# Softmax values computed with the tokens on the partitions, at the head of each attention layer

## The chip, the cores and the metric

The kernel runs on one core of one Trainium2 chip. The metric is the device time of one execution in microseconds (us). A core has TensorE (PE in the profile, its weight loads PEld), VectorE (DVE), ScalarE (ACT), GpSimd (POOL) and SyncE (SP), which here only issues DMAs.

## The reference

A transformer trunk of two layers on 512 tokens of width 1024, in float32:

```python
for l in range(DEPTH):                              # 2
    h = rmsnorm(x, attn_norm[l])
    sb_q, sb_k, sb_v, df_q, df_k, df_v = jnp.split(h @ w_in[l], splits, axis=-1)   # six times 512 columns
    sb_out = stick_breaking_attention(sb_q, sb_k, sb_v)          # 8 heads of 64
    dq, dk = rope(df_q, pos), rope(df_k, pos)
    df_heads = differential_attention(dq, dk, dvv, lam)          # 4 heads: two softmax maps of 64, values of 128
    df_out = rmsnorm(df_heads, subln_norm[l]) * (1.0 - lambda_init)
    x = x + concat([sb_out, df_out]) @ w_o[l]
    h = rmsnorm(x, mlp_norm[l])
    x = x + square(relu(h @ w_ff1[l])) @ w_ff2[l]                # 4096 wide
return rmsnorm(x, final_norm)
```

## The kernel before, in words

**Numbers in two parts.** Every float32 operand of a matmul is split into a high part, which ACT rounds, and a low part, which DVE gets by subtraction (`split`, `W.split_part`, `make_h`). A product of two such operands is a *triple* of matmuls: high times high, high times low, low times high (`three`, lines 278 to 283). The weights' splits show in the profile as `whi` (L116) and `wlo` (L117), the activations' as `h_hi` (L228) and `h_lo` (L229).

**Layout.** x lies transposed, with the 1024 features in eight chunks on the partitions and the 512 tokens along the free axis. `h` is x times the norm's gain only; the factor per token of the RMS norm is multiplied in when a projection leaves PSUM. For that, `add_sq` squares the chunks (ACT) and sums them (DVE) into `ssq`; `rms_a` transposes `ssq` on PE (`rs_a`), reduces it to `rcol`, one factor for each token on the partitions, and `rms_b` spreads it (`rb_a`) to `rbc`, the same factors along the free axis of all partitions. Cosine and sine tables are multiplied with `rbc` once.

**Weights.** They come in units of 128x1024, through a ring of three raw buffers filled by SP's queue in the order of `_UNITS`, and are split into one of two slots (four in the MLP). A unit's split can begin when its slot's former unit has been used up.

**Projections.** `dense` walks through `ORDER`. Item `d` is one softmax head's query and key (two units), `s` two stick-breaking heads' query and key, `u` the values of two stick-breaking heads and `w` those of one softmax head. Each unit gives a *block*: eight triples, one for each chunk, with the weights stationary and 512 tokens moving, into one PSUM bank. So a value block has features on the partitions; `evict_v` multiplies it with `rbc` (DVE), transposes it on PE (L374, `vT`), and splits it (L381, L382) into `vs` or `vd_hi`, `vd_lo`, which attention reads with tokens on the partitions.

**The opening of a layer.** In layer 0, the two units of `d0` are computed chunk by chunk as x arrives, into two banks. In layer 1, x's chunks come out of layer 0's MLP, where they lie with tokens on the partitions: `back` transposes a chunk on PE (L872, `yT`), adds it to x (L873, DVE) and makes `h`; then the same two units of `d0` are computed chunk by chunk (lines 1023 to 1041), with the squares behind them.

**Order.** Instructions go to each engine's queue in an order that a scheduler derives at compile time from the order of the program, letting later ready instructions pass. Within an attention layer the program's order is made by a planner (lines 729 to 747): it keeps a clock of estimated PE time, 0.648 us a triple, and after every dense triple spends a credit on pieces of attention (`attn`): scores S, transposes T of the weights, outputs O, for 8 units of softmax heads and then 16 of stick-breaking heads. Credit is what is left of attention (`ATT`, 54 us) over what is left of the dense work (`DENSE`, 145 us), at most `CAP`. Attention may touch a head `DLY_R` + `DLY_D` (3.5 + 8 us) after a `d` block's eviction, `DLY_S` (6 us) after an `s` block's. These delays stand for the splits and for the small DMAs that copy queries and keys into stacks (`move`, L408, on SP's queue: twelve for a `d`, six for an `s`). Steps count triples: `rms_a` is issued at step `RA`, `rms_b` at `RB`; before `RB` no block is evicted, and the blocks are held in PSUM. The dense work ends with `wo(1)`, the half of the output projection that reads softmax heads; `wo(0)`, which reads the stick-breaking heads, comes when attention is done.

**MLP.** Four groups; in each, eight blocks `f` and then seven sums of matmuls ("forms", with two banks each), which are a Strassen scheme for the second matrix. PSUM has eight banks, given out under four tags: `t` 2, `mm` 2, `s` 3, `o` 1.

Of the kernel before, what the change touches and what calls it, by code (L numbers as in the profile page):

```python
# [30 lines left out]
ORDER = ("d0", "w0", "d1", "w1", "d2", "w2", "d3", "w3", "s0", "u0", "s1", "u1", "s2", "u2", "s3", "u3")  # L31
# [5 lines left out]
RA, RB, DLY_V = (21, 20), (32, 31), 3.5  # L37
# [3 lines left out]
TAIL, ATT, DENSE, CAP = 6.0, 54.0, 145.0, 0.1  # L41
# [8 lines left out]
def _unit_list():  # L50
# [5 lines left out]
    for l in range(L):  # L56
        for item in ORDER:
            b = int(item[1])
            if item[0] == "d":
                units.append(("x", l, b, 0))  # L60
                units.append(("x", l, b, 1))
            elif item[0] == "s":
                qk(l, SBQ, SBK, b)
            else:
                units.append(("p", l, (SBV if item[0] == "u" else DFV) + b * P))
# [86 lines left out]
def trunk(ctx, tc, xT, w, w2, gains, gfin, lamv, cos, sin, out):  # L152
# [39 lines left out]
    W.loaded = 2  # L192
    W.load(3)
# [103 lines left out]

    def constants(a2):
# [18 lines left out]
    for l in range(L):  # L317
        with ExitStack() as actx:
# [27 lines left out]
            if l == 0:  # L346
                for c in range(KC):
                    if c % 2 == 0:
                        for i in range(2):
                            W.split_part(i, c * P, (c + 2) * P)  # L350
                    opened = make_h(c, gcol("attn", 0, c))
                W.split = 2
                for i in range(2):
                    W.home[2 + i] = tuple(
                        m[:, 2 * i : 2 * i + 2, :].rearrange("p e t -> p (e t)") for m in (md_hi, md_lo))
                squares = [add_sq(c, c == 0, tt, nc.vector) for c in range(KC)]
# [4 lines left out]
                W.do_split(3)  # L361
                behind(squares[2][0], W.last[0])
                behind(squares[2][1], W.last[1])
                W.do_split(4)
                constants(a2)

            def evict_v(pt, kind, b, which):
# [3 lines left out]
                def rest():  # L371
                    tv = bank("s" if kind == "u" else "t", f"vT{l}{kind}{b}")
                    for tb in range(4):
                        nc.tensor.transpose(tv[:, tb * P : (tb + 1) * P], t[:, tb * P : (tb + 1) * P], ident)  # L374
                    if kind == "u":
                        hi, lo = (vs[:, :, 2 * b : 2 * b + 2, a : a + 64] for a in (0, 64))
                        src = tv.rearrange("p (t h e) -> p t h e", t=4, h=2)
                    else:
                        hi, lo = (v[:, :, b * P : (b + 1) * P] for v in (vd_hi, vd_lo))
                        src = tv.rearrange("p (t e) -> p t e", t=4)  # L380
                    nc.scalar.activation(hi, src, AF.Copy)  # L381
                    nc.vector.tensor_tensor(out=lo, in0=src, in1=hi.bitcast(F32), op=ALU.subtract)  # L382
                    ready[("vs" if kind == "u" else "vd", b)] = clock[0] + 1.5

                defer(DLY_V, rest)

# [311 lines left out]
            def dense():  # L698
                pts = opened_by.pop() if l else None
                if l == 0:  # L700
                    us = [W.next("x"), W.next("x")]
                    pts = [bank("mm", f"p{l}{i}") for i in range(2)]
                    turns = [(c, i) for c in range(5) for i in range(2)] + [(c, i) for i in range(2) for c in (5, 6, 7)]
                    for c, i in turns:
                        three(pts[i], wpair(us[i], c), hpair(c), c == 0, c == KC - 1)
                        yield 3 * 0.216
                step, b = 2 * KC, int(ORDER[0][1])
                held = [(pts[0], "d", b, "q"), (pts[1], "d", b, "k")]
                for item in ORDER[1:]:
                    kind, b = item[0], int(item[1])  # L710
                    for which in ("qk" if kind in "ds" else "v"):
                        name = f"p{l}{kind}{b}{which}"
                        for pt in block(name, "s" if step in (16, 24, 32) else "mm"):
                            step += 1
                            if step == RA[l]:
                                dgs["a"] = rms_a(ssq, 1.0 / D, rcol, f"a{l}", nc.vector, tr)
                            if step == RB[l]:
                                rms_b(rbc, f"a{l}", dgs["a"])
                                nc.vector.tensor_mul(cos_t, cos_t, rbc)
                                nc.vector.tensor_mul(sin_t, sin_t, rbc)  # L720
                            yield 3 * 0.216
                        held.append((pt, kind, b, which))
                        if step >= RB[l]:
                            for args in held:
                                {"w": evict_v, "u": evict_v, "s": evict_s, "d": evict_d}[args[1]](*args)
# [4 lines left out]
            done = 2 * KC * 3 * 0.216 if l else 0.0  # L730
# [27 lines left out]
        with ExitStack() as fctx:  # L758
# [89 lines left out]

            def turned(tb, j):
# [61 lines left out]
            for g in range(GROUPS):  # L911
# [12 lines left out]
                for k in range(2 * GP):  # L924
                    for n, pt in enumerate(block(f"f{l}_{g}_{k}", "any")):
# [12 lines left out]
                for f, form in enumerate(FORMS):  # L938
                    to = [bank((("s", "s"), ("s", "o"), ("mm", "mm"))[f % 3][r], f"{form}{l}{g}{r}") for r in range(2)]
# [5 lines left out]
                    for n, (c, i, r) in enumerate(work):  # L945
# [76 lines left out]
            else:  # L1022
                W.pools.pop()
                us = [W.next("x"), W.next("x")]
# [83 lines left out]
```

## Time and profile before

| | us |
|---|---|
| median of 3 runs | 1175.3 (1173.34 to 1177.56) |
| the profiled execution | 1172.68 |
| its span, first to last instruction | 1170.9 |
| TensorE busy in it | 1147.6 |
| VectorE busy | 813.1 |
| ScalarE busy | 651.5 |
| GpSimd busy | 212.7 |

Rows of a timeline read: start, duration (both us), engine, line, operation, what it writes and reads, shape, count, and in brackets the idle time of the engine before it with what ended it. A merged row with "x2" covers two instructions. Matmuls overlap, so that a single one lasts longer than the distance to the next. Rows of waits read: who waited, for whom, us in total, times, longest. In the chain of work, a piece is counted only for the time in which it holds up the end.

### The profile page before, as it was taken

Reading aid. Unit: us, or ns where it says so; the run is one execution under the profiler, and the core shown is the slowest. Engines: PE = TensorE matmul, PEld = TensorE weight load, DVE = VectorE, ACT = ScalarE, POOL = GpSimd, SP = SyncE. Lnnn points to the kernel's source line nnn. Section 1 sums busy time; section 2 is a strip of 40 time slices with the busy share of each in tenths; the row PEclk is TensorE's granted clock in tenths of the full one; section 3 lists DMA queues with packets and bytes.
Section 4 is the critical chain, followed back from the end, with each engine's and each line's share of the span. In section 5 each row is a group of like instructions: output and inputs, shape, how many; then the busy total and the mean of one; then the engine's idle time right before and its main releaser. Section 6 shows DMA issues by size and latency. Waiting matters only on the chain.

```text
span 1170.9 us, 15335 instructions
## 1 busy us (share of the span) xinstructions
PE 1147.6 (98%) x5454; PEld 951.2 (81%) x5454; DVE 813.1 (69%) x1302; ACT 651.5 (56%) x1153; POOL 212.7 (18%) x282
## 2 busy tenths in 40 slices
PE   9999999999999999999899999999999999999996
PEld 6787888888888888888677878888888888888885
DVE  7888788765545746647778887877664466475568
ACT  6455666556656446455445555655666564554554
POOL 1222443130100101002012215331201010010021
PEclk9999999999999999999999999999999999999999
DMA  7555333255844936727416553432548357276185
GB/s 243 158 156 172 119 116 108 72 189 153 196 149 108 229 123 125 222 96 159 106 54 190 153 161 109 125 110 72 216 120 224 128 127 228 93 148 210 36 175 132
DMA packets 56860, 170.11 MB, mean 145 GB/s; under 512 B 7120, under 2 KB 8144, under 8 KB 56784
## 3 DMA queue, kind: packets, MB, share of 16 engines
q1 hardware_dynamic: 46416, 131.88, 34.0%
q0 software_dynamic: 10224, 37.23, 18.0%
q8 instruction: 43, 0.70, 0.2%
q14 instruction: 33, 0.27, 0.1%
q10 hardware_dynamic: 144, 0.02, 0.0%
HBM read 138.17 MB, written 2.10 MB: 120 GB/s over the span
## 4 chain that ended last, share of the span: by engine, by line
PE 86%; DVE 5%; DMA 2%; issue 2%; ACT 1%; POOL 0%; SPq 0%; POOLq 0%; DVEq 0%; ACTq 0%
PE f L283 10%; PE f L281 10%; PE f L282 10%; PE x L281 4%; PE x L283 4%; PE x L282 4%; PE wo L281 3%; PE wo L283 3%; PE wo L282 3%; DMA q<-in_w 2%; DVE wlo L117 1%; PE T1s L555 1%; PE T0s L555 1%; PE O0s L584 0%; PE O1s L584 0%
## 5 line engine op out<-in xcount | busy, mean ns | idle before, releaser
L117 DVE TENSOR_TENSOR wlo<-raw,whi 128x1024 fp32r<-128x1024 f32 (+1 forms) x132 | 157.0, 1193 | 95.6 <-ACT whi L116 95.0
L117 DVE TENSOR_TENSOR wlo<-q,whi 128x512 fp32r<-128x512 f32 x224 | 145.9, 687 | 108.6 <-ACT whi L116 108.1
L281 PE MATMUL f<-h_hi,whi 128*128 128x512 f32 x512 | 199.6, 390 | 0.0
L283 PE MATMUL f<-h_hi,wlo 128*128 128x512 f32 x512 | 199.3, 389 | 0.0
L282 PE MATMUL f<-h_lo,whi 128*128 128x512 f32 x512 | 199.2, 389 | 0.0
L116 ACT ACTIVATE whi<-q 128x512 fp32r<-128x512 f32 x224 | 129.4, 624 | 123.7 <-DMA q<-in_w 45.4
L116 ACT ACTIVATE whi<-raw 128x1024 fp32r<-128x1024 f32 (+1 forms) x132 | 133.9, 1019 | 111.7 <-PE f L282 55.0
L783 POOL DMA_DIRECT2D q<-in_w x64 | 56.0, 882 | 557.1 <-DVE wlo L117 471.3
L283 PEld LDWEIGHTS f<-h_hi,wlo 128*128 128x128 f32 x512 | 96.1, 188 | 20.1
L282 PEld LDWEIGHTS f<-h_lo,whi 128*128 128x128 f32 x512 | 96.1, 188 | 20.0
L281 PEld LDWEIGHTS f<-h_hi,whi 128*128 128x128 f32 x512 | 96.1, 188 | 19.7
L225 DVE TENSOR_TENSOR Al<-F,Ah 128x256 fp32r<-128x256 f32 (+2 forms) x96 | 74.8, 779 | 44.1 <-ACT Ah L224 44.0
L281 PE MATMUL x<-whi,Ah 128*128 128x512 f32 x256 | 100.0, 391 | 0.0
L282 PE MATMUL x<-wlo,Ah 128*128 128x512 f32 x256 | 99.8, 390 | 0.0
L283 PE MATMUL x<-whi,Al 128*128 128x512 f32 x256 | 99.7, 389 | 0.0
L224 ACT ACTIVATE Ah<-F 128x256 fp32r<-128x256 f32 (+2 forms) x96 | 67.6, 704 | 45.7 <-DVE F L819 43.7
L282 PEld LDWEIGHTS x<-wlo,Ah 128*128 128x128 f32 x256 | 48.1, 188 | 10.3 <-DVE wlo L117 0.5
L283 PEld LDWEIGHTS x<-whi,Al 128*128 128x128 f32 x256 | 48.1, 188 | 10.0
L281 PEld LDWEIGHTS x<-whi,Ah 128*128 128x128 f32 x256 | 48.1, 188 | 9.8
L810 ACT ACTIVATE F<-f 128x512 f32<-128x512 f32 x64 | 37.5, 587 | 10.8 <-DVE Al L225 5.4
L811 ACT ACTIVATE F<-F 128x512 f32<-128x512 f32 x64 | 40.4, 631 | 1.5
L228 ACT ACTIVATE h_hi<-x,g_all 128x512 fp32r<-128x512 f32 x32 | 22.5, 718 | 26.6 <-DVE x L692 13.8
(1059 smaller groups left out, 2566.5 us busy)
## 6 DMA issues: line engine op xcount, KB each, us to landing
raw<-in_w SPq DMA_DIRECT2D x126, 512.0 KB, 3.6
q<-in_w SPq DMA_DIRECT2D x64, 512.0 KB, 5.5
q<-in_w POOLq DMA_DIRECT2D x64, 512.0 KB, 5.9
x<-in_xT SPq DMA_DIRECT2D x8, 256.0 KB, 4.6
raw<-in_w SPq DMA_DIRECT2D x8, 128.0 KB, 4.5
yx<-y POOLq DMA_DIRECT2D x2, 512.0 KB, 8.0
y<-y POOLq DMA_DIRECT2D x2, 512.0 KB, 7.5
y<-yx POOLq DMA_DIRECT2D x2, 512.0 KB, 5.3
```

Source lines behind the costliest of these rows:

```text
L116: h = nc.scalar.activation(hi[:, a:b], raw[:, a:b], AF.Copy)
L117: self.last = h, nc.vector.tensor_tensor(out=lo[:, a:b], in0=raw[:, a:b], in1=hi[:, a:b].bitcast(F32), op=ALU.subtract)
L224: nc.scalar.activation(hi, src, AF.Copy)
L225: nc.vector.tensor_tensor(out=lo, in0=src, in1=hi.bitcast(F32), op=ALU.subtract)
L228: a = nc.scalar.activation(h_hi[:, c, :], x[:, c, :], AF.Copy, scale=g)
L281: nc.tensor.matmul(pt, ah, bh, start=first, stop=False)
L282: nc.tensor.matmul(pt, ah, bl, start=False, stop=False)
L283: nc.tensor.matmul(pt, al, bh, start=False, stop=last)
L555: nc.tensor.transpose(pt[:, off : off + P], u["w"][qi][:, kb * P : (kb + 1) * P], ident)
L783: nc.gpsimd.dma_start(t, quad(g, q, c), accum_op=ALU.add)
L810: nc.scalar.activation(t, pt, AF.Relu)
L811: nc.scalar.activation(t, t, AF.Square)
```

## The change

The values of the four softmax heads are no longer blocks `w` of a projection. At the head of each attention layer, `opening` computes all of them at once, with `h` stationary and the weights moving: for each of the eight chunks, four triples (one for each 128 tokens) of 512 columns, into four banks (three `s`, one `o`). The result has tokens on the partitions and needs no transpose; `evict_values` scales it by `rcol` and splits it. In layer 0 this runs as x and the weights arrive, in halves of units; in layer 1 chunk by chunk behind `came`, which prepares one chunk ahead, with its square and its sum. `d0` becomes an ordinary item, `ORDER` changes, the steps of the norm are set anew for each layer, `CAP` rises to 0.3, and the bank tags in the MLP are other ones.

```diff
-ORDER = ("d0", "w0", "d1", "w1", "d2", "w2", "d3", "w3", "s0", "u0", "s1", "u1", "s2", "u2", "s3", "u3")
+ORDER = ("d0", "d1", "d2", "u0", "d3", "u1", "s0", "s1", "u2", "s2", "u3", "s3")
-RA, RB, DLY_V = (21, 20), (32, 31), 3.5
+RA, RV, RB, DLY_V = (24, 37), (32, 43), (36, 47), 3.5
-TAIL, ATT, DENSE, CAP = 6.0, 54.0, 145.0, 0.1
+TAIL, ATT, DENSE, CAP = 6.0, 54.0, 145.0, 0.3
...
+        for j in range(KC // 2):
+            units.append(("v", l, j))
...
-    raws = [wraw.tile([P, 1024], F32, tag="raw", name=f"raw{i}") for i in range(2)]
+    raws = [wraw.tile([P, 1024], F32, tag="raw", name=f"raw{i}") for i in range(3)]
     for c in range(KC):
         nc.sync.dma_start(x[:, c, :], xT[c])
-        if c % 2 == 0:
-            for i in range(2):
-                nc.sync.dma_start(raws[i][:, c * P : (c + 2) * P], w[i][:, c * P : (c + 2) * P])
+        if c < 6:
+            part = slice(c % 2 * 512, c % 2 * 512 + 512)
+            nc.sync.dma_start(raws[c // 2][:, part], w[c // 2][:, part])
...
+    def opening(l, ahead=None):
+        pts = [bank("o" if tb == 3 else "s", f"pv{l}{tb}") for tb in range(4)]
+        for n in range(KC):
+            c = CAME[n] if l else n
+            if ahead:
+                ahead(n)
+            if n % 2 == 0:
+                u = W.next("v")
+            for tb in range(4):
+                rs = slice(tb * P, tb * P + P)
+                three(pts[tb], (h_hi[:, c, rs], h_lo[:, c, rs]), wpair(u, n % 2, 512), n == 0, n == KC - 1)
+                yield pts
...
+            def evict_values(pts):
+                for tb, pt in enumerate(pts):
+                    r = rcol[:, tb : tb + 1]
+                    nc.scalar.activation(vd_hi[:, tb, :], pt, AF.Copy, scale=r)
+                    nc.vector.scalar_tensor_tensor(
+                        out=vd_lo[:, tb, :], in0=pt, scalar=r, in1=vd_hi[:, tb, :].bitcast(F32),
+                        op0=ALU.mult, op1=ALU.subtract)
+                for b in range(4):
+                    ready[("vd", b)] = clock[0] + 4.0
...
-                        for pt in block(name, "s" if step in (16, 24, 32) else "mm"):
+                        for pt in block(f"p{l}{kind}{b}{which}", "s" if step == 48 else "mm"):
...
+            def came(n):
+                h = back(CAME[n])
+                s = add_sq(CAME[n], n == 0, ft, nc.vector)
+                behind(s[0], h[0])
+                if n:
+                    behind(s[1], h[1])
+                return s
...
-                    for n, pt in enumerate(block(f"f{l}_{g}_{k}", "any")):
+                    for n, pt in enumerate(block(f"f{l}_{g}_{k}", ("s", "s", "mm", "s", "mm", "s", "s", "s")[k])):
...
-                    to = [bank((("s", "s"), ("s", "o"), ("mm", "mm"))[f % 3][r], f"{form}{l}{g}{r}") for r in range(2)]
+                    to = [bank((("mm", "mm"), ("s", "s"), ("s", "o"))[f % 3][r], f"{form}{l}{g}{r}") for r in range(2)]
...
                         if tail and not last and n == 5:
-                            for c_ in CAME[:2]:
-                                back(c_)
+                            squares = [came(0)]
...
-                us = [W.next("x"), W.next("x")]
-                pts = [bank("mm", f"p{l + 1}{i}") for i in range(2)]
                 for tb in (0, 1):
                     add_to(tb, 0, to[tb])
-                for c in CAME[2:4]:
-                    back(c)
-                for n, c in enumerate(CAME):
-                    if n in (2, 3):
-                        for c_ in (CAME[4:6], CAME[6:])[n - 2]:
-                            h = back(c_)
-                    for i in range(2):
-                        three(pts[i], wpair(us[i], c), hpair(c), n == 0, c == CAME[-1])
-                squares = [add_sq(c, n == 0, ft, nc.vector) for n, c in enumerate(CAME)]
...
+                for pts in opening(1, lambda n: n + 1 < KC and squares.append(came(n + 1))):
+                    pass
                 opened_by.append(pts)
```

More of the change, by code (lines that the diff above doesn't have):

```diff
@@ L355, in trunk @@
                         m[:, 2 * i : 2 * i + 2, :].rearrange("p e t -> p (e t)") for m in (md_hi, md_lo))
+                for c in range(KC):
+                    if c == 6:
+                        W.load(4)
+                    W.split_part(c // 2, c % 2 * 512, c % 2 * 512 + 512)
+                    opened = make_h(c, gcol("attn", 0, c))
+                W.split = 4
+                W.load(6)
                 squares = [add_sq(c, c == 0, tt, nc.vector) for c in range(KC)]
@@ L729, in trunk @@
             at = attn()
[L730 removed]
+            done = 4 * KC * 3 * 0.216 if l else 0.0
             spent = credit = 0.0
```

70 lines of the change are left out of this document (30 added, 40 removed).

## The prediction

> **What bounds the kernel now.** I read the page first (engines, chain), then the busy time by stage, then TensorE's waits, then the timeline at the places that the diff touches.
>
> ```profile
> span 1170.9 us, 15335 instructions
> PE 1147.6 (98%) x5454; PEld 951.2 (81%) x5454; DVE 813.1 (69%) x1302; ACT 651.5 (56%) x1153; POOL 212.7 (18%) x282
> ...
> PE 86%; DVE 5%; DMA 2%; issue 2%; ACT 1%; POOL 0%; SPq 0%; POOLq 0%; DVEq 0%; ACTq 0%
> ```
>
> TensorE is busy for 98% of the span and carries 86% of the chain that ends last. So only two things pay: fewer instructions on PE, and fewer PE waits. The table of stages says where waits are left (columns: stretch, length, then busy time of PE, its weight loads, DVE, ACT, POOL; granted clock, DMA share, GB/s).
>
> ```profile
> core 0: us, PE busy (x) PEld busy (x) DVE busy (x) ACT busy (x) POOL busy (x), PEclk, DMA share, GB/s
> 5.20:29.30 24.10, 23.80 (x102) 18.76 (x100) 19.93 (x45) 15.32 (x27) 2.06 (x1) 1.00 0.78 270
> 29.30:107.20 77.90, 75.41 (x383) 62.41 (x383) 67.39 (x144) 39.25 (x93) 17.36 (x12) 1.00 0.56 163
> 107.20:249.00 141.80, 141.80 (x767) 120.47 (x766) 111.70 (x165) 87.61 (x171) 51.84 (x80) 1.00 0.34 108
> 249.00:574.00 325.00, 324.96 (x1436) 268.73 (x1435) 195.37 (x285) 178.76 (x279) 33.37 (x37) 1.00 0.61 159
> 574.00:609.30 35.30, 30.20 (x145) 23.49 (x144) 28.63 (x43) 15.51 (x24) 1.80 (x7) 1.00 0.22 75
> 609.30:687.40 78.10, 74.85 (x381) 61.99 (x381) 67.64 (x144) 40.55 (x96) 16.45 (x12) 1.00 0.57 162
> 687.40:829.00 141.60, 141.60 (x766) 120.29 (x765) 111.69 (x165) 86.21 (x168) 51.67 (x80) 1.00 0.35 108
> ```
>
> The second half of each attention layer and the MLP leave PE no idle time. Idle are 5.1 us between layer 0's MLP and layer 1's first blocks, and 2.5 and 3.25 us in the softmax halves (29.3 to 107.2, 609.3 to 687.4), where DVE is 87% busy. TensorE's own waits name the causes:
>
> ```profile
> PE yT L872 <- DVE x L873: 1.9, 1, 1.9
> PE yT L872 <- DVE yx L866: 1.6, 2, 1.3
> PE S1d L465 <- DMA kl1d3k<-hl1d3k: 1.5, 1, 1.5
> PE p1d2q L281 <- ACT whi L116: 1.4, 1, 1.4
> PE S0d L465 <- issue: 1.4, 1, 1.4
> PE p1w0v L283 <- DVE wlo L117: 1.2, 1, 1.2
> ```
>
> **The change, part by part.**
>
> **1. The transposes of the softmax values go.** Four value blocks a layer, each 24 matmuls and four transposes, become 32 triples, which is 96 matmuls of the same 512 columns: the matmul count stays, 2 x 16 transposes go.
>
> ```profile
> 17.86 0.39 PE L281 MATMUL p0w0v<-h_hi,mdh 128*128 128x512 f32 x1
> ...
> 23.30 0.39 PE L281 MATMUL p0d1q<-h_hi,mdh 128*128 128x512 f32 x1
> ...
> 46.30 0.44 PE vT0w L374 x4
> ...
> L374 PE MATMUL vT0w<-edge,tv0w x16: 270/272/301, 35.7 to 94.9; 128*128 128x128 f32 x16
> ```
>
> The 24 matmuls of w0 take 23.30 - 17.86 = 5.44 us, 0.227 us each. On the chain, four transposes hold PE for 0.44 us, though each lasts 0.272 us; they overlap. I take the chain's figure: 8 groups x 0.44 = **3.5 us**. The Trainium skill, in "TensorE: Matmul & The Clock Gate", Part 4: PE-mode transpose, gives about 275 ns for a transpose inside a kernel; the 272 ns here agree with it as a duration. By that figure the 32 would be worth 8.8 us; the chain's row decides against it.
>
> Off PE: per layer, 4 DVE products with `rbc`, 4 ACT copies and 4 DVE subtractions become 4 ACT copies with a per-token scale and 4 DVE scale-and-subtracts. That is 4 DVE instructions fewer; cost nothing: it lies under the matmuls of d0, and the four banks are not asked for before block d1q (step 48) and the first scores. Without that cover, ACT and DVE would need about 3 us in a row (four each of the 0.72 and 0.74 us rows quoted under 3).
>
> **2. Layer 0's opening.** Each arriving chunk of x now feeds 12 matmuls (2.72 us) instead of 6.
>
> ```profile
> 1.36 4.45 PE L206 MATMUL warm<-edge 128*128 128x512 bf16 x10 [1.36 <-POOL edge L200]
> ...
> 5.11 0.42 ACT L116 ACTIVATE whi<-raw 128x256 fp32r<-128x256 f32 x1 [0.30 <-DMA raw<-in_w]
> ...
> 5.24 0.99 PE L281 MATMUL p<-h_hi,whi 128*128 128x512 f32 x1
> ...
> 23.53 0.60 PE L248 MATMUL rs_a<-edge,ssq 128*128 128x128 f32 x4
> ...
> 29.37 0.47 PE L274 MATMUL rb_a<-dgha,ones_r 128*128 128x512 f32 x1
> ```
>
> Now the 48 matmuls from 5.24 to 17.86 take 12.6 us instead of 10.9: 1.7 us lost in waiting. SP issues 8 x-chunks and 6 weight halves of 256 KB instead of 8 and 8 of 128 KB, then unit 3: per chunk 512 KB in 2.72 us is 193 GB/s, under the 270 GB/s that this stretch moves already, so DMA hides behind PE; cosine and sine queue behind three more weight loads, but are needed only at step 36. The first split is 512 wide, between 0.42 us and twice that after 5.11: PE starts at 5.5 to 5.95, I take 5.8. Of the 1.7 us I keep 0.5 (bounds 0 and 1.7; the first operands are still late, later chunks no longer). `rs_a`, now at 23.53, is due after 24 triples, at 22.6: if the squares are no earlier than now, chunk 6, queued behind it on PE, waits up to 0.9 us, inside these bounds. 5.8 + 0.5 + 96 x 0.227 = 28.1. The same 96 matmuls now end at 29.37 less 0.4 for the `rs_a` transposes, 28.9. **0.8 us** gained (-0.4 to 1.6).
>
> **3. Layer 1's opening.** Now 48 matmuls on two banks, then block w0 stalls because the units of both halves of d0 hold both weight slots until their last matmul. After: four banks, units used one after the other, one chunk (`came`) prepared ahead, and squares and their sums moved in between.
>
> ```profile
> 578.92 0.40 PE L283 MATMUL x<-whi,Al 128*128 128x512 f32 x1
> ...
> 579.33 1.22 DVE L117 TENSOR_TENSOR wlo<-raw,whi 128x1024 fp32r<-128x1024 f32 x1
> ...
> 580.46 1.28 DVE L873 TENSOR_TENSOR x<-x,yT 128x512 f32<-128x512 f32 x2
> 581.18 1.34 ACT L228 ACTIVATE h_hi<-x,g_all 128x512 fp32r<-128x512 f32 x2 [4.93 <-DVE x L873]
> ...
> 588.30 0.74 DVE L229 SCALAR_TENSOR_TENSOR h_lo<-x,g_all,h_hi 128x512 fp32r<-128x512 f32 x1
> ...
> 597.66 0.69 DVE L238 TENSOR_TENSOR ssq<-ssq,spare 128x512 f32<-128x512 f32 x1
> ...
> 609.34 0.39 PE L281 MATMUL p1d1k<-h_hi,whi 128*128 128x512 f32 x1
> ```
>
> The first chunk's chain is DVE's queue, which the diff leaves as it is: `wlo` to 580.5, x, then `h_hi` done at about 581.9. Before it the two yT waits of 1.6 us stay. Then 96 matmuls (21.8 us) and the transposes of six more chunks (2.6 us; the second chunk's fit into the wait): 606.3. The same work now ends at 609.34 less 0.85 for `rs_a` and `rb_a`: 608.5. A chunk takes PE 2.72 + 0.44 = 3.16 us; DVE has 0.64 + 0.74 + 0.69 + half of 1.22, 2.7 us: fits, narrowly, and ACT (0.72, a square, half a split) easily. I take **2.0 us** gained. If each chunk's chain (0.44 + 0.64 + 0.72 + 0.74) has one 1.22 us split ahead of it, it is 3.76 against 3.16 us: 0.6 x 6 = 3.6 lost, so the bounds are -1.6 and 2.2.
>
> **4. The softmax half.** d0's eviction now waits for step 48 (48 x 0.648 = 31.1 us of the planner's time) instead of step 32, so attention starts 10 us later and d0 to d3 are each taken as soon as the planner calls them ready, 11.5 us after their eviction. Bounds: all idle there goes, 5.7 us; or d1 and d2 meet in both layers the wait of 1.4 and 1.5 us that d3's scores show (copies on SP's queue behind weight loads), 5.8 us lost. The eviction burst after `rbc` is shorter (no w blocks held, values read out earlier), which speaks for the p1d2q wait to go; d3's I keep. **1.0 us** gained.
>
> **5. The end of attention.** s3 comes last; u3, which lay behind it, comes before.
>
> ```profile
> 184.64 0.48 PE L281 MATMUL p0u3v<-h_hi,whi 128*128 128x512 f32 x1
> ...
> 194.19 0.28 PE L465 MATMUL S0s<-st0s3k,st0s3q 128*128 128x256 f32 x1
> ...
> 194.20:224.60 30.40, 30.40 (x177) 26.19 (x176) 24.33 (x34) 17.60 (x35) 7.26 (x16) 1.00 0.19 68
> ...
> 224.32 0.28 PE L584 MATMUL O0s<-zl,vs 128*128 128x256 f32 x1
> ...
> 226.64 0.69 DVE L225 TENSOR_TENSOR vdl<-mt,vdh 128x512 fp32r<-128x512 f32 x1 [0.70 <-ACT vdh L224]
> 227.19 0.39 PE L281 MATMUL wo<-vdh,whi 128*128 128x512 f32 x1
> ```
>
> Now 9.6 us pass from s3's last matmul to its first scores (eviction, copies), 30.3 more to the last O. After the change PE has left from there: `wo(1)`, 96 x 0.227 = 21.8 us, and attention pieces of 10.4 planner us (four units of s3 7.2, trailing ones 3.2), 10.9 us: 32.7 us, against 39.9 now. The 30.3 must shrink to 23; the busiest engine in it, DVE, has 24.3, of which part can move forward into the 9.6. At the very end the planner leaves no `wo(1)` triple between the last O and `wo(0)`, where now 2.7 us lie (224.4 to 227.19) over a split that ends at 227.33. Bounds per layer 0 and 7.3 us; nearest the DVE figure: **0.5 us lost** a layer, 1.0.
>
> **6. Without cost.** Other bank tags in the MLP: PE idles 0.04 us in 249 to 574, and a form's banks have 5.4 us of matmuls to be emptied in; without that cover it would be the two adds per form. POOL's queue gains and loses nothing.
>
> Sum: 3.5 + 0.8 + 2.0 + 1.0 - 1.0 = **6.3 us**. The profiled execution, 1172.7 us (span 1170.9), lies 2.6 below the median of 1175.3, so 1166.4 for such a one and 1169.0 as a median. Under 0.3% (3.5 us) a measurement of this kernel can't tell from no change.
>
> **The rivals.**
> A, the forecast: 1169.0, its own range 1166 to 1171.5; 0.50.
> B, the softmax halves lose d3's waits too, since u0 and u1 frame d3: 2.9 more plus the rest of p1d2q's kind, 1 us: 1165. The 87% DVE load speaks against it; 0.15.
> C, one chunk ahead is too little in layer 1 (the lower bound of 3): 6.3 - 3.6 = 2.7, 1172.6. DVE's 81% in 574 to 609 speaks for it, the single 1.22 us split per two chunks against; 0.14.
> D, the other side: s3's chain doesn't shrink. 39.9 against 32.7 us is up to 7.2 a layer, 14.4 - 7.3 = 7.1 slower: 1182.4. It decides from 5.4 us a layer (then 3.5 slower). For it: scores, sigmoid, scan and O run in turn, seven score buffers; against: PE was never idle there, so the present 30.3 us are no lower bound; 0.15.
> E, PE falls to half clock. In layer 1's opening PE idles from about 579.15 (four transposes fewer before the last matmuls, four behind them) to 581.9, 2.75 us; with one more 1.22 us split ahead, 4.0. The ten cold matmuls in the rows of 2 take 0.445 us each, 0.22 over the warm pitch; ten such cost 2.2, with the split 3.4: 1172.4. All stretches above show a clock of 1.00, with waits up to 1.9 us; 0.06.
> The Trainium skill, "TensorE: Matmul & The Clock Gate", Part 1, has the clock halved after an idle window of about 3.4 us; by that rule E needs the one split more; no run here shows such a gap.
>
> **How the numbers follow.** Faster by over 0.3% holds A and B with a little of C and E: 0.67. Within 0.3%: the rest of C and E: 0.17. Slower: D and a worse C: 0.16. The range runs from 1162 (below B) to 1178, which takes in C, E and the milder half of D; about 0.15 stays outside.
>
> **What the profile after would show.** No vT0w or vT1w group, vT0u as before. In 574 to about 606 idle PE of 4 us or less, and no wait at the first block behind the opening; under C, a wait of about 0.6 us before each chunk. PE idle of 4 to 5 us in the two softmax halves together. Between the last O and `wo(0)` under 1 us of idle; under D several. If PE idle in sum falls by less than 2 us, the forecast is wrong even if the transposes are gone.

## The result, and the profile after

The changed kernel takes 1182.11 us (median of 6 runs, 1179.91 to 1185.22) against 1174.75 us (6 runs, 1172.57 to 1177.56) of the kernel before, run beside it: a ratio of 1.0068, 95% interval 1.0052 to 1.0083. It is about 8 us slower, where 6.3 us of gain were predicted. The profiled execution took 1181.12 us, with a span of 1179.4 us, 8.5 more than before. From the first part of the page:

```profile
span 1179.4 us, 15247 instructions
PE 1148.4 (97%) x5422; PEld 951.4 (81%) x5422; DVE 816.8 (69%) x1292; ACT 653.2 (55%) x1151; POOL 220.7 (19%) x282
...
PE 77%; DVE 8%; DMA 4%; issue 4%; ACT 3%; POOL 3%; SPq 1%; POOLq 0%; ACTq 0%; DVEq 0%
```

The 32 transposes are gone from the count of TensorE (5454 to 5422), and yet its busy time is no lower, and its share of the chain fell from 86 to 77%: what TensorE waits for got longer. The table of stages, with the columns of the prediction, first the last 40.9 us of the kernel before (its attention stands in the prediction), then the kernel after (layer 0's attention in two halves, layer 1's opening, layer 1's attention in two halves, the last 40.9 us):

```profile
1130.00:1170.90 40.90, 30.11 (x144) 24.52 (x142) 29.40 (x47) 19.54 (x40) 7.42 (x10) 0.95 0.66 153
```

```profile
28.10:117.90 89.80, 86.00 (x422) 70.81 (x422) 72.03 (x149) 43.05 (x97) 18.45 (x12) 1.00 0.52 147
117.90:254.80 136.90, 132.77 (x712) 112.04 (x710) 110.76 (x159) 84.42 (x166) 55.54 (x80) 0.99 0.35 104
580.00:611.80 31.80, 28.30 (x137) 22.60 (x137) 26.04 (x37) 14.80 (x22) 0.76 (x6) 1.00 0.24 83
611.80:699.40 87.60, 85.64 (x427) 71.03 (x426) 72.56 (x152) 45.01 (x100) 19.86 (x13) 1.00 0.54 157
699.40:835.20 135.80, 131.43 (x712) 110.94 (x711) 109.22 (x160) 83.36 (x165) 53.98 (x80) 1.00 0.35 105
1138.50:1179.40 40.90, 29.06 (x133) 23.47 (x131) 27.47 (x44) 18.40 (x38) 6.56 (x9) 0.89 0.62 144
```

Idle TensorE (length less busy) in the softmax halves is what it was in sum: 3.8 and 2.0 us after, 2.5 and 3.25 before. In the halves behind them, where there was none, there are now 4.1 and 4.4 us. (Cut where the first scores of a stick-breaking head begin, at 117.31 and 697.49 before and at 126.77 and 708.20 after, the idle times are the same.) In the last 40.9 us the work done fell from 144 to 133 matmuls, at a lower clock. The places where whole blocks of work begin give the account: the first matmul of `d0` behind layer 0's opening, and the first `f` of each MLP.

| | before | after | change of the piece |
|---|---|---|---|
| end of the same work in layer 0's opening (96 matmuls and `rs_a`) | 29.37 | 28.16 | -1.2 |
| layer 0's MLP begins | 248.95 | 254.80 | +7.1 behind the opening |
| layer 1's opening, from the sixth triple of `x4` in its last group | 33.7 long | 31.4 long | -2.3 |
| layer 1's MLP begins | 829.13 | 835.00 | +2.5 behind the opening |
| end of the span | 1170.9 | 1179.4 | +2.6 |

(The 31.4 and 33.7 us end with the same work too: behind the 96 matmuls after, and at 608.5 before, where the prediction put the equal work.) So the openings gained a little more than was predicted, and attention, with the transposes of the softmax values taken out of it, still grew by 9.6 us; what follows layer 1's attention added 2.6. What TensorE waited for, after:

```profile
PE xT L883 <- DVE y L889: 3.5, 1, 3.5
PE T0s L575 <- DVE fl0d L226: 2.5, 1, 2.5
PE T1s L575 <- DVE fl1d L226: 2.1, 1, 2.1
...
PE S0d L485 <- DMA kl0d2k<-hl0d2k: 1.4, 1, 1.4
```

The two longest new ones, one in each layer, are `T0s` and `T1s`: at the changeover from softmax to stick-breaking heads they wait over 2 us for `fl0d` and `fl1d`, the low part of the last softmax weights (these steps read the PSUM bank that the next transposes go to). Here is what stands ahead of that step in layer 0, on POOL and on DVE (rows of the timeline, after):

```profile
140.17 1.92 POOL L260 TENSOR_TENSOR rc<-ms,mhalf 128x4 f32<-128x4 f32 x1 [0.16 <-DVE ms L254]
142.44 1.81 POOL L265 TENSOR_TENSOR dghd<-edge,chi 128x512 fp32r<-128x512 f32 x1 [0.35 <-PE S0s L486]
```

```profile
140.01 1.22 DVE L119 TENSOR_TENSOR wlo<-raw,whi 128x1024 fp32r<-128x1024 f32 x1
142.12 0.17 DVE L261 CAST chi<-rc 128x4 fp32r<-128x4 f32 x1 [0.90 <-POOL rc L260]
142.20 1.22 DVE L503 TENSOR_TENSOR_SCAN C0s<-keep0s,edge 128x512 f32<-128x512 f32 x1
143.33 0.94 DVE L262 TENSOR_TENSOR clo<-rc,chi 128x4 f32<-128x4 f32 x1
144.19 0.68 DVE L226 TENSOR_TENSOR hl0s1q<-t0s1k,hl0s1q 128x512 fp32r<-128x512 f32 x1
144.79 0.68 DVE L226 TENSOR_TENSOR fl0d<-T0d,fh0d 128x512 fp32r<-128x512 f32 x1
...
145.62 0.52 PE L575 MATMUL T0s<-edge,sig0s 128*128 128x128 f32 x3 [2.55 <-DVE fl0d L226]
```

and the same steps before:

```profile
130.54 1.01 POOL L259 TENSOR_TENSOR rc<-ms,mhalf 128x4 f32<-128x4 f32 x1
```

```profile
131.58 0.17 DVE L260 CAST chi<-rc 128x4 fp32r<-128x4 f32 x1 [1.14 <-POOL rc L259]
131.79 0.16 DVE L261 TENSOR_TENSOR clo<-rc,chi 128x4 f32<-128x4 f32 x1
131.87 1.22 DVE L483 TENSOR_TENSOR_SCAN C0s<-keep0s,edge 128x512 f32<-128x512 f32 x1
133.00 0.66 DVE L225 TENSOR_TENSOR fl0d<-T0d,fh0d 128x512 fp32r<-128x512 f32 x1
```

`rc` is the power in a norm of a softmax head's output (`rms_a`), on POOL; DVE splits its column (`chi`, `clo`), and everything behind these two short steps in DVE's queue waits with them. In the changed kernel a 1.22 us `wlo` runs beside the power, which takes 1.92 instead of 1.01 us, and `clo`, 0.16 us before, lasts 0.94 us until POOL's `dghd` has ended at 144.25. From the start of the power to the start of `fl0d` it is 4.62 us, before 2.46; 0.6 of the difference is the step `hl0s1q`, which now stands ahead of `fl0d`. The Trainium skill, "SBUF — State Buffer", Who interferes with whom, has a DVE instruction with two inputs in SBUF contend with a GpSimd instruction that reads SBUF, over ports that only one of them can hold; both pairs here agree with it (the power ends 0.86 us behind `wlo`'s end, `clo` ends with `dghd`).

### The profile page after: what moved, and what is told of

Same layout as the page of the kernel before. It is cut to its first block, busy times and chain, and to the rows that moved or that the text cites. A ratio compares the mean times of both kernels' runs of the same rounds, so it can differ in the third digit from the quotient of the medians.

```text
span 1179.4 us, 15247 instructions
## 1 busy us (share of the span) xinstructions
PE 1148.4 (97%) x5422; PEld 951.4 (81%) x5422; DVE 816.8 (69%) x1292; ACT 653.2 (55%) x1151; POOL 220.7 (19%) x282
## 4 chain that ended last, share of the span: by engine, by line
PE 77%; DVE 8%; DMA 4%; issue 4%; ACT 3%; POOL 3%; SPq 1%; POOLq 0%; ACTq 0%; DVEq 0%
PE f L282 10%; PE f L284 10%; PE f L283 10%; PE x L282 4%; PE x L284 4%; PE x L283 4%; PE wo L282 2%; PE wo L284 2%; PE wo L283 2%; DMA q<-in_w 2%; PE pv L282 1%; PE pv L284 1%; PE pv L283 1%; SPq L428 1%; DVE wlo L119 1%
## 5 line engine op out<-in xcount | busy, mean ns | idle before, releaser
L119 DVE TENSOR_TENSOR wlo<-raw,whi 128x1024 fp32r<-128x1024 f32 (+1 forms) x128 | 160.8, 1258 | 99.9 <-ACT whi L118 99.3
L506 POOL TENSOR_TENSOR sig0s<-sig0s,C0s 128x128 f32<-128x128 f32 (+3 forms) x32 | 28.7, 897 | 50.7 <-DVE C0s L503 34.3
```

Source lines behind the costliest of these rows:

```text
L119: self.last = h, nc.vector.tensor_tensor(out=lo[:, a:b], in0=raw[:, a:b], in1=hi[:, a:b].bitcast(F32), op=ALU.subtract)
L506: nc.gpsimd.tensor_mul(sig[:, 0:wd], sig[:, 0:wd], C[:, 1 : wd + 1])
```

## The experiments

Four theories stood at the start. ORDER: the new sequence of blocks sets the copies and splits of the heads against each other. CAP: the planner's higher cap lets saved-up attention follow a triple in larger bunches. START: attention begins some 10 us later, so the same attention is packed into less time. CHAIN: the norm chain just shown. All runs below have a median and a ratio to the kernel before, run on the same chip beside them.

| run | kernel, edit | median, us | ratio, 95% interval |
|---|---|---|---|
| e1_order | after, old `ORDER` | 1181.71 | 1.0062 (1.0038 to 1.0085) |
| e2_late | before, `d0` offered 10.4 us later | 1177.99 | 1.0045 (1.0027 to 1.0062) |
| e3_cap03 | before, `CAP` 0.3 | 1186.99 | 1.0131 (1.0104 to 1.0157) |
| e4_chi | after, `chi`, `clo` on POOL | 1175.13 | 1.0007 (0.9996 to 1.0019) |
| e7_cap01 | after, `CAP` 0.1 | 1183.76 | 1.0059 (1.0041 to 1.0078) |
| e6_tags | after, old bank tags in the last MLP | 1182.99 | 1.0053 (1.0033 to 1.0073) |
| e8_capchi | e4 and e7 together | 1182.12 | 1.0044 (1.0030 to 1.0059) |
| e9_bchi | before, `chi`, `clo` on POOL | 1187.24 | 1.0083 (1.0056 to 1.0109) |
| e10_chi3 | e4 for the third norm alone | 1179.67 | 1.0044 (1.0029 to 1.0060) |
| e11_chinot3 | e4 for all others | 1178.36 | 1.0034 (1.0020 to 1.0048) |
| e5_ordcap | after, old `ORDER` and `CAP` 0.1 | 1174.29 | 0.9987 (0.9968 to 1.0007) |
| e12_chicap02 | e4 with `CAP` 0.2 | 1178.76 | 1.0039 (1.0018 to 1.0060) |
| e14_border | before, new `ORDER` | 1183.77 | 1.0071 (1.0044 to 1.0098) |
| e13_ordcaptags | e5 with the old tags | 1173.52 | 0.9985 (0.9970 to 1.0001) |
| e15_ordcapchi | e5 with `chi`, `clo` on POOL | 1167.60 | 0.9929 (0.9903 to 0.9954) |
| e16_octchi | e15 with the old tags | 1169.62 | 0.9946 (0.9926 to 0.9966) |

**One part undone or done alone: e1 to e4.**

```diff
 e1, on after:  -ORDER = ("d0", "d1", "d2", "u0", "d3", "u1", "s0", "s1", "u2", "s2", "u3", "s3")
                +ORDER = ("d0", "d1", "d2", "d3", "s0", "u0", "s1", "u1", "s2", "u2", "s3", "u3")
 e2, on before: -    ready[(kind, b)] = clock[0] + DLY_D
                +    ready[(kind, b)] = clock[0] + DLY_D + (10.4 if b == 0 else 0.0)
 e3, on before: -TAIL, ATT, DENSE, CAP = 6.0, 54.0, 145.0, 0.1
                +TAIL, ATT, DENSE, CAP = 6.0, 54.0, 145.0, 0.3
 e4, on after:  -nc.vector.tensor_copy(chi, col)
                -nc.vector.tensor_sub(clo, col, chi.bitcast(F32))
                +eng.tensor_copy(chi, col)      # POOL for the norms of the softmax heads' outputs
                +eng.tensor_sub(clo, col, chi.bitcast(F32))
```

> The changed kernel (1182.1 us), with the order of before without its w blocks: d0 to d3 in a row, then s0 u0 s1 u1 s2 u2 s3 u3. By the planner's arithmetic s0's scores then come at 99.0 planner us instead of 106.8 (before: 97.7), and u3 lies behind s3 again. ORDER theory (the 8 us lost against the plan come from d3 behind u0 and from s3 last): about 1173 to 1175, the wait of T0s for fl0d (2.5 us) and the half clock behind it gone. START theory (they come from attention starting 10 planner us later, which the values at the head force): within 2 us of 1182, waits of the same size between 100 and 150 us. CHAIN theory (a chance meeting of DVE and POOL at the changeover from softmax to stick-breaking heads): anything that moves the changeover removes that one wait with its half clock, some 4 us in layer 0 and 2 to 3 us in layer 1: 1175 to 1178.

> The kernel before (1174.8 us), in which only the planner calls d0 ready 10.4 planner us later, so that attention starts as late as in the changed kernel. START theory: slower by 5 to 8 us, 1180 to 1183, with waits for fl0d or for copies at the changeover. ORDER and CHAIN theories: within 2 us of before.

> The kernel before with CAP 0.3 alone. CAP theory (pieces of attention in pairs, closer together, outrun DVE): slower by 4 us or more, with waits behind DVE among the stick-breaking heads. ORDER, START and CHAIN theories: within 2 us of 1174.8.

> The changed kernel, in which the two small instructions chi and clo of the softmax heads' norm run on POOL, behind POOL's pow, so that DVE no longer waits for POOL there. CHAIN theory: T0s no longer waits 2.5 us (2.1 in layer 1) for fl0d, and no half clock follows: 1182.1 less 6 to 8, 1174 to 1176. ORDER and START theories: the wait moves to another link, 1179 to 1182.

ORDER seemed to fall: with the old order nothing came back. CHAIN missed there too: e1 has no wait for `fl0d` or `fl1d` left, and is not faster. START was right in kind, with less than its 1180 to 1183: the later offer alone costs the kernel before 0.45%, about 5 us, and its new waits are for POOL's `sig0s` and `sig1s` (1.4 us each), not for `fl0d` or copies. CAP alone cost the kernel before 1.3%, 15 us (13 between the medians). Waits of TensorE in e3, none of which the kernel before has:

```profile
PE S1d L465 <- DMA kl1d2k<-hl1d2k: 1.9, 1, 1.9
...
PE S0d L465 <- DMA kl0d2k<-hl0d2k: 1.6, 1, 1.6
...
PE S1s L466 <- DMA kl1s3k<-hl1s3q: 1.2, 1, 1.2
PE T0s L555 <- DVE fl0s L225: 1.2, 1, 1.2
```

The pieces reach copies and splits that are not there yet. On e4, CHAIN looked confirmed: the waits for `fl0d` and `fl1d` fell to 0.2 and 0.3 us, and the time by 7 us.

**Cap and tags on the changed kernel, and a control: e6 to e9.** e7 sets `CAP` back, e8 does that and e4's edit, e9 makes e4's edit on the kernel before. e6 gives the last layer's MLP its old bank tags:

```diff
-block(f"f{l}_{g}_{k}", ("s", "s", "mm", "s", "mm", "s", "s", "s")[k])
+block(f"f{l}_{g}_{k}", "any" if last else ("s", "s", "mm", "s", "mm", "s", "s", "s")[k])
-to = [bank((("mm", "mm"), ("s", "s"), ("s", "o"))[f % 3][r], ...
+to = [bank(((("s", "s"), ("s", "o"), ("mm", "mm")) if last else (("mm", "mm"), ("s", "s"), ("s", "o")))[f % 3][r], ...
```

> The changed kernel with the planner's cap of 0.1 instead of 0.3, all else as changed. On the kernel before, the cap of 0.3 alone cost 13 us. CAP (the cap costs the changed kernel the same): 1182.1 - 13 = 1169, at least faster than 1176. START (attention begins 10 planner us later, and the larger cap is what catches it up): with 0.1 about 4.45 planner us of attention are left behind the last projection in each layer, so that cap's gain is given back: 1178 to 1184. CHAIN (the split of the second half's norm on DVE behind a slow pow on POOL) is not touched by the cap: the wait of T0s for fl0d stays at 2 us or more in both layers.

> The changed kernel with the bank tags of before in the last layer's MLP. TAGS (the new tags delay the last transposed outputs): the wait of the last matmul group for y falls from 3.5 us to 2.6 or less and TensorE keeps its full clock behind it, a gain of 1 to 2.4 us: 1179.7 to 1181. Rival: the wait is that of the chain from the last sum of squares, whatever the banks: 3.0 to 3.8 us again, 1182.

> The changed kernel with both the cap of 0.1 and the split of the norm's column (chi, clo) on POOL. If the cap and the chain cost independently: 1175.1 less what the cap alone gives (up to 13 us), so 1163 to 1170, faster than both kernels. If the cap's 0.3 is needed after the later start (START): 1174 to 1178, no gain over the split alone.

> The kernel before with the split of the norm's column (chi, clo) on POOL, as the control of the same edit on the changed kernel. CHAIN (the wait comes from the changed order alone; before, fl0d was never late): 1174.0 to 1175.5, no change. Rival (the edit is a gain of its own, whatever the order, since it takes two steps from DVE's queue): 1168 to 1172, and then the 7 us that it gave on the changed kernel do not speak for the chain as the cause.

Setting the cap back gave nothing (e7), as START had it and CAP had not; the waits for `fl0d` and `fl1d`, which CHAIN had staying, are gone in e7. With the cap back the split on POOL gave nothing measurable either (e8 against e7; in e8 `rb_d` waits 3.0 us for POOL), and 1182.1 lies outside both of e8's ranges. e7's long waits are others than those of after; `rs_m` is the sum of squares at the head of the MLP, late because the last head now is:

```profile
PE S0d L485 <- DMA st0d3q<-hl0d3k: 2.5, 1, 2.5
PE rs_m L960 <- POOL ssq L239: 2.0, 2, 1.4
```

e6's wait for y fell to 2.7 us, near the 2.6 of TAGS, but the clock behind it still fell (0.61), and the time did not move. On the kernel before, e4's edit costs 0.83%, 10 us (e9), which neither expectation had. Its two longest waits, and POOL's rows in layer 0:

```profile
PE S1d L465 <- DMA kl1d3k<-hl1d3k: 5.2, 1, 5.2
PE S0d L465 <- DMA kl0d3k<-hl0d3k: 4.7, 1, 4.7
```

```profile
84.37 2.01 POOL L259 TENSOR_TENSOR rc<-ms,mhalf 128x4 f32<-128x4 f32 x1
...
87.91 1.35 POOL L266 TENSOR_TENSOR dgld<-edge,clo 128x512 fp32r<-128x512 f32 x1
89.22 1.29 POOL L441 TENSOR_TENSOR u0d3q<-u0d3q,v0d3k 128x512 f32<-128x512 f32 x1
```

Before, POOL did `u0d3q` (a step of `d3`'s rotation) in the gap in which it waited for DVE's `chi`, from 85.55; now its norm runs through and `u0d3q` starts 3.7 us later. SP, in order, then issues a weight load (at 92.47) right ahead of eight of `d3`'s copies (from 93.12), where before it had gone 2.1 us ahead of them (89.90 and 91.96); the copies `kl0d3k` land 4.8 us after their issue instead of 2.7, and TensorE waits 4.7 us for them. So the edit is no gain of its own.

**Where does e4's gain lie, and do the planner's two settings belong together: e10, e11, e5, e12.** e10 and e11 let `name in ("d02", "d12")`, the third norm of each layer, choose POOL, or all norms but these; e5 sets both `ORDER` and `CAP` back; e12 is e4 with a cap of 0.2.

> The changed kernel with the split of the norm's column (chi, clo) on POOL for the third norm of each layer alone, the one whose slow pow (1.92 us) held DVE's queue at the changeover to the scan heads. CHAIN (what the edit on all norms gained, 7 us, came from that one place): waits of T0s and T1s for fl0d, fl1d under 0.5 us and 1174 to 1177. Rival (the gain was a general one, from 18 short steps less on DVE): 1179 to 1182.

> The complement: the split on POOL for all norms that POOL serves but the third of each layer. CHAIN: the waits of T0s and T1s for fl0d, fl1d stay at 2 us or more and the time at 1180 to 1184. Rival (general gain): 1175 to 1178.

> The changed kernel with both settings of the planner as before: the softmax heads' blocks, then s and u in turn, and the cap of 0.1. What is left of the change are the values by tokens, the two openings and the later start. START (the later start alone loses what the parts 1 to 3 gain): 1174 to 1178. If the loss lies in order and cap together (each alone gave nothing back): 1168 to 1172. If the loss needs neither (every variant of the opening shows 36 to 38 us of idle PE): 1180 to 1184.

> The changed kernel with the split on POOL for all of POOL's norms and a cap of 0.2, between the 0.3 (1175.1) and the 0.1 (1182.1) measured with the same split. If the cap acts by how much attention is left at the end: between the two, 1175 to 1182. If each cap only moves pieces onto other waits, by chance: anything from 1170 to 1184, with waits at other places than either neighbour.

CHAIN as I had it fell: in e10 the two waits are 0.6 us each, but only 0.24% of e4's 0.61% comes back, and e10's interval overlaps that of the changed kernel; in e11 the waits are still there (1.9 and 2.3 us) and 0.34% comes back, between the two ranges. The two about add up, so the chain at the changeover is at most a part of e4's gain, not all of it. e12 lies between its neighbours of 0.1 and 0.3, as if the cap worked by degrees, but its longest waits in attention are for the copies of d2 and d3 (`st0d2q` 2.3, `kl0d3k` 2.2 us), where its neighbours wait less (e4 1.5 for d2, e8 1.7 for d3), and its runs spread from 1174 to 1184; it decides nothing.

e5 decides: with both settings back, 0.81% returns, 9.5 us, though neither alone returns anything. It ends just inside START's range (1174 to 1178), so what the openings gained is still lost somewhere. e5's first MLP begins at 249.48 and its second at 826.32, against 254.80 and 835.00. What TensorE still waits for in its attention:

```profile
PE T0s L575 <- DVE fl0s L226: 1.3, 1, 1.3
PE T1s L575 <- DVE fl1d L226: 1.0, 1, 1.0
PE T0s L575 <- DVE fl0d L226: 0.9, 1, 0.9
PE S1d L485 <- DMA st1d0q<-hl1d0k: 0.9, 1, 0.9
```

**Each setting by itself on a kernel that starts early, and a better version: e14, e13, e15, e16.** e14 gives the kernel before the new order, with its `w` items in their places (`... "d2", "w2", "u0", "d3", "w3", "u1", "s0", "s1", "u2", "s2", "u3", "s3"`).

> The kernel before with the changed order of blocks alone (u0 behind d2 and w2, u1 behind w3, s0 and s1 together, s3 last), its cap of 0.1 kept. If order and cap each are enough to lose what the two together lose on the changed kernel (7 to 9 us, not additive): 1181 to 1185. If the order alone is harmless and only the later start makes it costly: 1174 to 1177.

> The changed kernel with the order of blocks, the cap and, in the last layer's MLP, the bank tags of before. Order and cap of before together gave 1174.3. TAGS: the wait of the last transposes for y falls from 3.6 us to 2.7 or less and the last layer's end loses 0.8 to 2.5 us less (the lower end if TensorE's clock is still halved behind the wait): 1171.8 to 1173.5, a little faster than before. Rival (the tags are worth nothing): 1174 to 1175.

> The changed kernel with order and cap of before, and the split of the norm's column on POOL. If that split takes away the waits for fl0d, fl0s, fl1d, fl1s that remain (1.1 + 1.5 + 1.1 + 0.9 us): 1170 to 1172. If POOL's delay pushes the third softmax head's copies behind a weight load, as it did on the kernel before: 1176 or more.

> All three together on the changed kernel: order and cap of before, the split of the norm's column on POOL, and the bank tags of before in the last layer's MLP. If split (1174.3 to 1167.6) and tags (1174.3 to 1173.5) add: 1166 to 1167.5, faster than both kernels. If the tags are worth nothing beside the split: 1167.6. If every such edit moves the waits anew: anything from 1167 to 1175.

The new order alone costs the kernel before 0.71%, 8 us, by these waits, 7.0 us in sum, none of which the kernel before has (against them, the waits for `d3`'s copies fall from 2.9 to 1.2 us):

```profile
PE rs_m L929 <- POOL ssq L238: 2.0, 2, 1.4
...
PE S0s L466 <- DMA kl0s0k<-hl0s0q: 1.4, 1, 1.4
PE S1s L466 <- DMA kl1s0k<-hl1s0q: 1.4, 1, 1.4
...
PE T0s L555 <- DVE fl0s L225: 1.1, 1, 1.1
PE T1s L555 <- DVE fl1s L225: 1.1, 1, 1.1
```

On the changed kernel the four combinations of order and cap are 1.0068 times the kernel before (new order, 0.3), 1.0062 (old, 0.3), 1.0059 (new, 0.1) and 0.9987 (old, 0.1). Undoing one gives nothing that can be measured, undoing both gives all. The profiled executions, one of each, show where, in us of the four pieces (the cuts are the first matmul of `d0` and the first `f` of each layer; before, the equal work at 29.37 and 608.5):

| | layer 0's opening | attention, both layers | layer 0's MLP and layer 1's opening | layer 1's MLP and the end | span |
|---|---|---|---|---|---|
| before | 29.4 | 440.2 | 359.6 | 341.8 | 1170.9 |
| after | 28.2 | 449.8 | 357.1 | 344.4 | 1179.4 |
| e1, old order | 27.9 | 447.0 | 360.3 | 344.7 | 1180.0 |
| e7, old cap | 28.1 | 447.4 | 359.5 | 345.1 | 1180.0 |
| e5, both | 28.2 | 441.3 | 356.8 | 344.5 | 1170.8 |
| e15, both, and the split on POOL | 28.0 | 436.2 | 358.7 | 345.8 | 1168.7 |

In attention one setting undone does give something, 2.8 or 2.4 us, against 8.5 for both. e1 and e7 lost that again in the third piece: both by a wait of 0.6 to 0.7 us at the head of the MLP (`rs_m`), e1 by a wait of 1.8 us for a split of weights (`whi`) at its end and a clock of 0.95 in 540 to 572, e7 by a clock of 0.74 and 0.83 in the 8 us from 584.3. So the two settings work together in attention, and losses elsewhere, half or more of them the clock's, hid what each alone had given.

With both set back, the split on POOL takes away all waits for `fl` (they are not in e15's list), and e15 is faster than both kernels: 1167.6 us, 0.9929 (0.9903 to 0.9954), a larger gain than the 2 to 4 us expected. Its second MLP begins at 822.86, 6.3 us earlier than that of the kernel before. The old tags add nothing that can be told apart (e13 beside e5, e16 beside e15; the intervals overlap), and in e16 the wait for y is 4.1 us in spite of them, so TAGS isn't borne out.

## Why the prediction was wrong

**The step that failed is attention behind the openings.** Parts 4 and 5 cancel in the sum (+1.0 and -1.0), so that with part 1 attention was to shrink by 3.5 us. It grew by 9.6. The half of the stick-breaking heads, which left TensorE no idle time before, was given no cost except at its very end; it has 8.5 us of idle time after. Of the two settings that arrange it, the cap was given no price and the order one for that end alone. Undoing both takes 8.5 of the 9.6 us away again (e5 against after, by piece) and 9.5 us of the time. TensorE's idle time in the span, whose fall by less than 2 us was the forecast's own sign of being wrong, rose from 23.3 to 31.0 us.

**Part 1, the transposes: right as far as seen.** 32 matmul records fewer, and no `vT0w`. Their price of 3.5 us was not measured alone. TensorE's busy time in attention is 1.5 us lower in e5 and 2.0 us lower in e15 than before, for work that differs by the 32 transposes alone; that hints at a price below 3.5.

**Parts 2 and 3, the openings: right, the first with some luck.** Layer 0's opening ends at 28.16 (28.1 predicted), layer 1's takes 31.4 us from the same point as before (31.5 predicted). The 28.1 left out the 0.4 us of `rs_a`, which stands inside the opening (at 25.43) after as well as before, and had TensorE start at 5.8, where it started at 5.25; the two cancel. The gain in layer 0 is thus 1.2 us, not 0.8, within the range given.

```profile
28.16 0.39 PE L282 MATMUL p0d0q<-h_hi,whi 128*128 128x512 f32 x1
...
611.88 0.39 PE L282 MATMUL p1d0q<-h_hi,whi 128*128 128x512 f32 x1
```

So rival C (one chunk ahead is too little) did not come about: idle in 580 to 611.8 is 3.5 us, and less than 4 was the mark.

**Part 4, the softmax half: the gain did not come.** Idle TensorE there was to fall from 5.7 us to between 4 and 5, and is 5.8. The waits for `whi` and `wlo` at `d2` went, as forecast, and `d3`'s, which were to stay, fell from 2.9 to 1.3 us; waits at d0 and d2 for copies (`kl0d2k` 1.4, `st1d0q` 0.9), of the kind that part 4 had as its lower bound, and for ACT and DVE took their place. That attention starts 10 us later was noted and given no price of its own; on the kernel before, the start alone costs some 5 us (e2).

**The cap and the order were not priced.** The diff raises `CAP` from 0.1 to 0.3, and the prediction speaks of it nowhere; alone on the kernel before it costs 15 us. Of the new `ORDER` only the end of attention was priced; alone it costs 8 us. On the changed kernel neither undone alone gives anything measurable, both give 9.5 us. This omission decided the sign: without the two settings, the changed kernel ends where the kernel before does (e5).

**Part 5, the end of attention: wrong in place and size.** A loss of 1.0 us was taken, and rival D was a stall behind s3's last matmul. In after there is no such stall, and no idle time between the last O and `wo(0)`, as forecast; the 4.1 and 4.4 us of the stick-breaking halves lie earlier, 2.5 and 2.1 of them at the changeover. With the old cap a wait at the MLP's head appears (e7: `rs_m` 2.0 us in two waits, the longer 1.4), a fifth of D's 7.2 a layer at most. What the new order costs the kernel before lies as much at the first stick-breaking heads (e14). D's total, 1182.4, is close to what was measured, by another way.

**Part 6, the bank tags: their part stays open.** The span behind the second MLP's beginning grew by 2.6 us, which the prediction had at nothing. Of that, 0.9 us is a longer wait for y (3.5 instead of 2.6 us), and 1.7 us the lower clock behind it: from the end of that wait to the end of the span it is 27.6 us, against 25.9 before and 26.0 in e4, which has the new tags and kept its clock. The tags do not decide the wait: with the old ones it is 2.7 us in e6, 1.9 in e13 and 4.1 in e16. POOL issues the last load of weights but one 0.9 us later behind `yx` than before, and the profile names no releaser; what sets the wait stays open.

**Rival E, the half clock, came at other places.** Layer 1's opening kept its clock of 1.00 in after; but behind waits of about the same size there (1.9 us, and 1.5 to 1.7 in two) the clock fell to 0.74 and 0.83 in e7 (8 us from 584.3) and to 0.81 and 0.76 in e15 (8 us from 576.7), so it was luck that it did not. What E's mechanism hit in after were waits that were not foreseen, as the section on the hardware shows. The six runs of after have a granted clock of 0.9938 in the mean, the 102 runs of the kernel before beside the experiments 0.9963: by an estimate from these, at most 3 of the 8 us (0.0025 x 1180) are lost to the clock.

**The sum, by piece.** The openings gained 1.2 and, with layer 0's MLP, 2.5 us (0.8 and 2.0 predicted), attention lost 9.6, the end lost 2.6: 8.5 us. In e5 the openings keep their gain and the end its loss (2.7 us), and attention is 1.1 us longer than before. With 1.5 to 3.5 us for the transposes, that leaves an estimated 2.5 to 4.5 us for the later start on the changed kernel, which no run has isolated there. B, that the softmax halves lose d3's waits, came true for d3 in part, but not for the sum of the waits.

## What to carry to other kernels

When a change moves where a planner starts interleaved work, the new start has a price, and so has each of the planner's constants in the diff; price them by what they do to the distance between a producer's copy and its reader. If undoing one suspect gives nothing back, undo two together before acquitting either, and compare the time piece by piece: here each of two gave 2.4 to 2.8 us in attention, which was lost again elsewhere, and both together 8.5. And an edit that is worth 7 us in one order can cost 10 in another, so a control on the kernel before belongs to each.

## What was not expected of the hardware

**Two engines hold each other up for whole instructions.** Of the 16 powers on POOL in layer 0 of before, after, e9 and e15, the four that take 1.84 to 2.01 us each began while `wlo` or the scan was under way on DVE, which read two operands from SBUF. The twelve that take 1.01 to 1.03 us began beside no step of DVE, one with a single input, or one with an operand in PSUM (`fl0d`); two of them had a scan beside them that began 0.2 and 0.9 us later. A 0.16 us step of DVE takes 0.94 us beside a product on POOL (rows above). A queue in order makes of such 0.9 us delays 2.5 us on TensorE.

**TensorE's clock can fall after waits of 2.3 to 2.5 us.** Stretches of about 4 us behind a wait, first of after (waits of 2.5 us at 145.6, 2.1 us at 726.6 and 3.5 us at 1151.8), then of e6 (2.5, 2.5 and 2.7 us), then of e4 (3.0 us); the clock is the third number from the end:

```profile
145.60:149.60 4.00, 3.98 (x13) 3.32 (x14) 2.64 (x4) 1.74 (x4) 2.24 (x6) 0.57 0.79 197
...
726.60:730.60 4.00, 4.00 (x23) 3.53 (x24) 2.58 (x4) 1.63 (x4) 2.88 (x8) 1.00 0.79 197
...
1151.80:1156.00 4.20, 4.20 (x17) 3.44 (x18) 3.01 (x5) 2.39 (x6) 1.42 (x2) 0.65 0.83 163
```

```profile
145.40:149.40 4.00, 3.72 (x13) 3.13 (x14) 2.90 (x5) 1.74 (x4) 2.39 (x6) 0.62 0.77 191
726.70:730.70 4.00, 3.78 (x13) 3.30 (x14) 2.89 (x5) 1.55 (x4) 1.96 (x5) 0.58 0.77 186
1152.40:1156.40 4.00, 3.94 (x15) 3.38 (x16) 3.07 (x6) 2.41 (x6) 1.49 (x2) 0.61 0.91 177
```

```profile
1147.50:1151.50 4.00, 3.83 (x21) 3.28 (x22) 3.19 (x6) 2.97 (x8) 1.59 (x2) 1.00 0.96 189
```

Each such stretch loses 1.5 to 1.7 us (4 us at 0.62 to 0.57) beside the wait itself. A wait of 3.0 us left the clock alone and one of 2.5 lowered it, as did one of 2.3 us in e11 (0.57 in 724.8 to 728.8), so the length does not decide by itself. At one place, the wait for y near the end, all 18 kernels can be compared: the six with waits up to 2.61 us kept 1.00 in the 4 us behind it and had 25.7 to 26.0 us left to the end; of the twelve with 2.64 to 4.11 us, two kept it (e4 3.05, e11 2.90; 26.0 us left), and ten fell to 0.50 to 0.66 and had 27.3 to 28.7 us left. The Trainium skill, "TensorE: Matmul & The Clock Gate", Part 1, has the clock halved after an idle window of about 3.4 us that runs freely; that the place in the window matters agrees with these rows, that a whole window of 3.4 us must be idle does not.
